# The place of ScalarE's high parts of U chunks, and the queue of one write of gates, in a decoder block with product-key experts

## The chip, the cores and the metric

The kernel runs on one core of a Trainium2 chip. The core has TensorE (PE, matmuls; its weight loads are shown apart as PEld), VectorE (DVE), ScalarE (ACT) and GpSimd (POOL), and SyncE (SP), which only issues transfers. Each engine takes its own instructions strictly in its order; semaphores join them. Transfers are issued from SP, ScalarE and GpSimd, each with its own queue. The metric is the device time of one execution in microseconds.

## The reference

One layer of a decoder: a normalised input goes through attention over a window beside gated linear attention, the sum is added to the input, and then comes the part that takes most of the time, an expert layer with product keys. Each of 512 tokens picks 16 of 16384 experts in each of 8 heads; an expert is one row of `u` and one of `v`.

```python
def block(args):
    xb, eb, gb = args                      # 128 tokens, their 128 experts, their 128 gates
    ub = jnp.take(u, eb, axis=0)
    hid = jax.nn.gelu(jnp.einsum('tkd,td->tk', ub, xb), approximate=False) * gb
    vb = jnp.take(v, eb, axis=0)
    return jnp.einsum('tk,tkd->td', hid, vb)
```

The expert indices and gates come from two top-16 searches over 128 keys each per head, the 16 best of their sums, and a softmax. At the end stands a last normalisation.

## The kernel before

**How the experts are computed.** The tokens are in four blocks of 128. For three of them (`DENSE`, 384 tokens) the kernel doesn't gather: it computes all 16384 experts with matmuls and multiplies by a dense matrix of gates that is zero where a token did not pick an expert. The last block (`GB`) is done by gathering rows, GpSimd fetching them (`gu`, `gv`) and DVE forming the products. 48 of the 384 tokens get their hidden values from gathered rows too (`spr`), so the U matmuls run over 336 tokens (`TU`).

**U chunks.** There are 128 chunks of 128 experts. A chunk c is loaded as float32 (two chunks to a transfer of 1 MB, tile `u`, a ring of three buffers), and `hilo` (L61) splits it: ScalarE writes the high part `uc<c>h` (L65), and DVE, or GpSimd early on, the low part `uc<c>l` (L66), source minus high part. Each has a ring of four buffers. `u_matmuls` (L697) does 24 matmuls (8 slices of the width, three products each: L70 high by high, L71 and L72 with the low parts) into one PSUM bank `ph`, of which there are two. `u_gelu` (L703) applies Gelu from that bank to `ge` (L706) and frees it; for the chunks of `AHEAD` the result goes to DRAM on ScalarE's queue (L708).

**Chunks ahead.** 88 of the chunks are in `AHEAD` and are computed before the V stage, in the order 4m, 4m+2, and from m = 20 on also 4m+1, 4m+3. The first 11 of them run during the search for experts, with a given engine for the low part (`lo_eng`). The others (`lo_eng` is None) are woven into the gate stage by `u_part` (L712). The last ones are, in this order, 116, 118, 117, 119, 120, 122, 121, 123, 124, 126, 125, 127. The other 40 chunks, odd ones from 1 on, run in the V stage.

**The gate stage.** It makes the matrix of gates. `gate_group` (L923) treats 16 tokens in two halves; for each half DVE builds one-hots (`o12`, L917, and `o2`, L935), TensorE does 24 matmuls into two banks `pg` (L942), and ScalarE evicts each bank to `gs` (L944). 24 groups make 48 halves, 96 evictions. In the third block (`SB`) ScalarE also copies the part for the first eight chunks to `gates_r[0]` (L949). After each odd group k the two groups in `gs` go to `Gd` in DRAM, 2 MB per write (L951): eleven writes on SP's queue and the last, k = 23, on GpSimd's. `woven` (L1186) strings the groups together with other work; in the last block it has, after groups 4 to 6, `dots_of` (two products with gathered rows on DVE) and, after groups 3 to 6, `ahead` (two fetches of such rows on GpSimd).

**The V stage.** From L1366, `prep(i)` prepares step i of the list `xs`, which begins with the U chunks 1, 3, 5, 7, 9 and then mixes V chunks and odd U chunks. For a U step it has ScalarE write the high part (L1372), runs `activate` (Gelu of gathered products), `gather_to(due[i])` (gathers and products up to a planned number, here the products of rows 6 and 7 at first), DVE's low part (L1385) and `loads(i)`. For a V step it multiplies the gates by the hidden values (L1377) and splits A and V in the same way (L1378, L1380, L1385, L1389); then 36 matmuls go into the six `acc` banks. `load_u` (L1300) loads two odd U chunks on SP's queue; three such loads stand before `prep(0)`.

**What sets the order.** DVE and GpSimd run in program order from the gate stage on (L1232). TensorE, ScalarE and SP are ordered by a scheduler's simulation up to L1246, and in program order after it; but their instructions of the V stage may be placed among the last ones of the gate stage. `tc.issue_after(ins)` adds no semaphore: each instruction traced within it on the engine of `ins` must come later than `ins` in that engine's order.

Of the kernel before, what the change touches and what calls it, by code (L numbers as in the profile page):

```python
# [12 lines left out]
AF = mybir.ActivationFunctionType  # L13
# [34 lines left out]
def peer_block_kernel(ctx: ExitStack, tc: tile.TileContext, a: dict, out: bass.AP):  # L48
# [663 lines left out]
    def u_part(c, lo_eng=None, after=None):  # L712

        j = c // 2 % 2
        if j == 0:
            u_load(c)
        uh, ul = hilo(u_part.raw[c % 2][:, j], [P, KD, P], f"uc{c}", lo_eng or nc.vector)
        with tc.issue_after(after.ins) if after is not None else nullcontext():
            ph, end = u_matmuls(c, uh, ul)
        u_gelu(c, ph)  # L720
        return end

    u_part.raw = {}

# [198 lines left out]
    def gate_group(bi, n, q):  # L923
# [5 lines left out]
        for t0 in range(0, TG, TB):  # L929
# [7 lines left out]
            for f in range(TB // 4):  # L937
                pt = bank(f"pg{n}{q}{t0}{f}", BK[f]).rearrange("p (a b) -> p a b", a=4)
                for i in range(4):
                    g, r = divmod(4 * f + i, 2)  # L940
                    for m in range(3):
                        nc.tensor.matmul(pt[:, i, :], o12[:, g, 0, :, r], o2[:, g, m, :, r],  # L942
                                         start=(m == 0), stop=(m == 2))
                nc.scalar.activation(gs[:, :, q % 2, :, t0 + 4 * f:t0 + 4 * f + 4].rearrange("p c i a -> p a c i"),  # L944
                                     pt.rearrange("p a (c i) -> p a c i", c=P // CG), AF.Copy)
            yield 1.68, 1.4
# [3 lines left out]
        if q % 2:  # L950
            (nc.gpsimd if k == NGRP - 1 else nc.sync).dma_start(Gd[:, :, k - 1:k + 1].rearrange("c p g e -> p c (g e)"),  # L951
                                                                gs.rearrange("p c g i t -> p c (g i t)"))

    gate_group.next = None
    gates_r = {}

# [214 lines left out]
    def chain(*gens):  # L1171
        for g in gens:
            yield from g
# [12 lines left out]
    def woven(n, rows, extra, rest=()):  # L1186
        for q in range(P // TG):
# [8 lines left out]
            if q in extra:  # L1196
                yield from chain(*extra[q])

    def breath():
# [166 lines left out]
    def prep(i, extra=()):  # L1366
# [14 lines left out]
        activate()  # L1381
        gather_to(due[i])
        for piece in extra:
            piece()
        nc.vector.tensor_tensor(l, src, h, OP.subtract)  # L1385
        if k == "u":
            ready[i] = h, l
# [100 lines left out]
    end = step["v", P - LAST]  # L1488
    prep(0)
    prep(1)  # L1490
    for i in range(end):
# [112 lines left out]
```

## Time and profile before

| | |
|---|---|
| median of 3 runs | 1478.58 us (1477.78 to 1479.39) |
| the profiled execution | 1486.71 us |
| its span, first to last instruction | 1484.9 us |
| mean granted TensorE clock in it | 0.989 |
| VectorE's waits for the gathered rows `gu`, `gv` | 8.1 and 5.2 us in all |
| evictions of gates (L944) | 96, 1110 ns each |
| Gelus of U chunks (L706) | 128, 440 ns each |
| high parts in the V stage (L1372), from the timeline | 1.06 us each |

A row of the page's groups reads: line, engine, operation, what it writes from what, count, then busy us, mean ns of one, idle time before it and who ended that. The profile is of one execution, which is longer than the runs without a profile. Roughly, attention and mixing take up to 280 us, the search for experts to 420 us, the gate stage to 800 us and the V stage the rest.

### The profile page before, as it was taken

What the parts mean: (1) busy time and instruction counts of PE and PEld (TensorE: products, weight loads), DVE (VectorE), ACT (ScalarE), POOL (GpSimd) and SP (SyncE); (2) the same over time, 40 slices, a digit from 0 to 9 for tenths busy, and PEclk for the clock granted to TensorE, in tenths of its full rate; (3) what the DMA queues carried; (4) which work ended last, traced back from release to release, by engine and by line L of the source; (5) the groups of instructions that cost most, each with busy time, mean ns of one, the idle gap of its engine ahead of it and who ended that gap; (6) DMA issues with size and microseconds to landing.
All of it is one profiled execution on the core that took longest, in us unless ns stands there. A gap on an engine that the chain in (4) does not pass through costs nothing.

```text
span 1484.9 us, 24692 instructions
## 1 busy us (share of the span) xinstructions
PE 1425.7 (96%) x9395; PEld 1268.4 (85%) x9395; DVE 1282.5 (86%) x2495; ACT 685.7 (46%) x1084; POOL 540.7 (36%) x374
## 2 busy tenths in 40 slices
PE   3999999899999999999998999999999999999997
PEld 3688777798899999999998888888888888888886
DVE  7577756769999899989885899999999999999997
ACT  5445475543344465555764433343333334333334
POOL 1000000044431444421022565666666657544520
PEclk9999899999999999999999999999999999999999
DMA  9262507344246899987789999999999999999971
GB/s 345 93 220 100 201 29 255 121 159 178 98 160 236 298 326 328 361 319 249 275 270 362 414 412 407 404 413 396 375 410 405 390 408 411 410 411 412 410 301 71
DMA packets 131607, 439.56 MB, mean 296 GB/s; under 512 B 13072, under 2 KB 51232, under 8 KB 110880
## 3 DMA queue, kind: packets, MB, share of 16 engines
q1 hardware_dynamic: 74080, 260.55, 46.3%
q0 software_dynamic: 44304, 161.50, 28.4%
q10 hardware_dynamic: 13104, 15.93, 3.0%
q8 instruction: 73, 1.20, 0.3%
q14 instruction: 46, 0.38, 0.1%
HBM read 393.36 MB, written 44.52 MB: 295 GB/s over the span
## 4 chain that ended last, share of the span: by engine, by line
PE 76%; DVE 9%; DMA 6%; issue 4%; ACT 2%; POOL 2%; SPq 0%; POOLq 0%; DVEq 0%; ACTq 0%
PE acc L70 11%; PE acc L71 11%; PE acc L72 11%; PE ph L70 8%; PE ph L72 7%; PE ph L71 7%; PE pg L942 3%; DMA u<-in_uT_dram 2%; POOL spr L1012 2%; DMA spr<-in_u_dram,spix 1%; PE pj L72 1%; PE pj L70 1%; PE pj L71 1%; PE pn L70 1%; PE pn L71 1%
## 5 line engine op out<-in xcount | busy, mean ns | idle before, releaser
L1064 POOL DMA_INDIRECT gu<-in_u_dram,ix_u x128 | 196.1, 1532 | 201.2 <-PE pg L942 89.3
L1099 POOL DMA_INDIRECT gv<-in_vP_dram,ix_v x128 | 193.8, 1514 | 153.1 <-DVE gu L1074 56.0
L1104 DVE SCALAR_TENSOR_TENSOR gacc<-gv,hg,gacc 128x1024 f32<-128x1024 f32 x127 | 162.5, 1280 | 5.4 <-DMA gv<-in_vP_dram,ix_v 5.2
L1074 DVE SCALAR_TENSOR_TENSOR gu<-gu,h2n 128x1024 f32<-128x1024 f32 x128 | 155.6, 1219 | 8.1 <-DMA gu<-in_u_dram,ix_u 8.1
L1012 POOL DMA_INDIRECT spr<-in_u_dram,spix x48 | 81.2, 1692 | 168.4 <-DVE spr L1018 127.2
L706 ACT ACTIVATE ge<-ph 128x336 f32<-128x336 f32 x128 | 56.3, 440 | 182.1 <-PE ph L72 176.7
L1380 ACT ACTIVATE Ah<-gr 128x384 fp32r<-128x384 f32 x128 | 66.9, 522 | 115.5 <-DVE gr L1377 111.7
L1158 POOL IOTA iot<- 128x256 bf16 x1 | 1.5, 1540 | 288.4 <-DVE h2Tl L681 288.4
L944 ACT ACTIVATE gs<-pg 128x512 f32<-128x512 f32 x96 | 95.3, 1110 | 2.5 <-PE pg L942 2.0
L935 DVE TENSOR_TENSOR o<-o,gp 128x3072 bf16<-128x3072 bf16 x48 | 84.1, 1753 | 4.7 <-PE pg L942 4.7
L942 PE MATMUL pg<-o,o 128*128 128x128 bf16 x1152 | 75.4, 221 | 0.0
L942 PEld LDWEIGHTS <-o 128*128 128x128 bf16 x1152 | 68.1, 98 | 4.9 <-issue 0.2
L1389 DVE TENSOR_TENSOR Al<-gr,Ah 128x384 fp32r<-128x384 f32 x128 | 70.7, 552 | 1.3 <-DMA Gd<-gs 1.3
L1018 DVE SCALAR_TENSOR_TENSOR spr<-spr,xs 128x1024 f32<-128x1024 f32 x48 | 58.5, 1220 | 10.9 <-DMA spr<-in_u_dram,spix 10.8
L917 DVE TENSOR_TENSOR o<-iot,t 128x2048 bf16<-128x2048 bf16 x48 | 58.3, 1219 | 4.2 <-PE pg L942 4.2
L218 DVE SCALAR_TENSOR_TENSOR macc<-wa,scs,macc 128x1024 f32<-128x1024 f32 x28 | 39.7, 1416 | 6.7 <-DMA wa<-in_w_ada_dram 6.5
L1377 DVE TENSOR_TENSOR gr<-gel,gr 128x336 f32<-128x336 f32 x64 | 32.2, 503 | 0.0
L71 PE MATMUL pq<-h2Tl,wq_0h 128*128 128x512 f32 (+1 forms) x80 | 28.2, 352 | 1.2 <-DVE h2Tl L681 1.2
L70 PE MATMUL pq<-h2Th,wq_0h 128*128 128x512 f32 (+1 forms) x80 | 28.3, 355 | 1.0 <-ACT qsc L769 1.0
L72 PE MATMUL pq<-h2Th,wq_1l 128*128 128x512 f32 (+1 forms) x80 | 28.7, 358 | 0.0
L70 PE MATMUL pq<-h2Th,wq_1h 128*128 128x512 f32 (+1 forms) x80 | 28.4, 355 | 0.0
L71 PE MATMUL pq<-h2Tl,wq_1h 128*128 128x512 f32 (+1 forms) x80 | 28.4, 355 | 0.0
(2591 smaller groups left out, 5035.7 us busy)
## 6 DMA issues: line engine op xcount, KB each, us to landing
u<-in_uT_dram SPq DMA_DIRECT2D x64, 1024.0 KB
v<-in_vP_dram SPq DMA_DIRECT2D x64, 1024.0 KB
gr<-Gd SPq DMA_DIRECT2D x15, 1536.0 KB
Gd<-gs SPq DMA_DIRECT2D x11, 2048.0 KB
wa<-in_w_ada_dram SPq DMA_DIRECT2D x20, 1024.0 KB
gsp<-ge ACTq DMA_DIRECT2D x88, 168.0 KB
gel<-gsp SPq DMA_DIRECT2D x32, 336.0 KB
wi<-in_w_in_dram SPq DMA_DIRECT2D x9, 1024.0 KB
```

The costliest lines, as they stand in the source:

```text
L70: nc.tensor.matmul(acc, lh, rh, start=start, stop=False)
L71: nc.tensor.matmul(acc, lh, rl, start=False, stop=False)
L72: return nc.tensor.matmul(acc, ll, rh, start=False, stop=stop)
L935: nc.vector.tensor_tensor(o2, o12[:, :, 1, None].to_broadcast([P, H, 3, P, 2]), gp3[:, g0:g0 + H, :, None].to_broadcast([P, H, 3, P, 2]), ...
L942: nc.tensor.matmul(pt[:, i, :], o12[:, g, 0, :, r], o2[:, g, m, :, r], start=(m == 0), stop=(m == 2))
L944: nc.scalar.activation(gs[:, :, q % 2, :, t0 + 4 * f:t0 + 4 * f + 4].rearrange("p c i a -> p a c i"), pt.rearrange("p a (c i) -> p a c i", ...
L1012: nc.gpsimd.indirect_dma_start(out=sp[m], out_offset=None, in_=a["u"], in_offset=bass.IndirectOffsetOnAxis(ap=sp["ix", i][:, j:j + 1], axi ...
L1064: nc.gpsimd.indirect_dma_start(out=ur, out_offset=None, in_=a["u"], in_offset=bass.IndirectOffsetOnAxis(ap=ix_u[:, s:s + 1], axis=0))
L1074: nc.vector.scalar_tensor_tensor(ur, ur, 1.0, h2n, op0=OP.mult, op1=OP.mult, accum_out=hid[:, s:s + 1])
L1099: nc.gpsimd.indirect_dma_start(out=vr, out_offset=None, in_=a["vP"], in_offset=bass.IndirectOffsetOnAxis(ap=ix_v[:, s:s + 1], axis=0))
L1104: nc.vector.scalar_tensor_tensor(gacc, vr, hg[:, s:s + 1], gacc, op0=OP.mult, op1=OP.add)
L1389: nc.vector.tensor_tensor(grp(Al), A, grp(Ah), OP.subtract)
```

## The change

There are four edits.

1. In `u_part`, when `lo_eng` is None and more than three Gelus have been recorded, the high part is traced under `issue_after` of the Gelu four back in the list `gelus`, to which each `u_part` adds its own.
2. `gate_group` keeps the second eviction of each half in `evicts`; `prep(0)` and `prep(1)` are traced under `issue_after(evicts[-2])`, which is the second eviction of the last half but one. That binds their ScalarE instructions, the high parts of chunks 1 and 3.
3. The write of gates for k = 21 (`NGRP - 3`) is issued on GpSimd's queue instead of SP's, and later in the program: `woven` pops it after the extra pieces of its group, so after two products on DVE and two fetches on GpSimd. The write for k = 23 stays where it was, as do the others.
4. In `prep`, `gather_to(due[i])` is left out at step 0 and comes after the low part at step 1. So the products of gathered rows 6 and 7 come after the low parts of chunks 1 and 3 on DVE, and their Gelu (`activate`) at the next step.

```diff
--- before.py
+++ after.py
@@ -714,12 +714,15 @@
         j = c // 2 % 2
         if j == 0:
             u_load(c)
-        uh, ul = hilo(u_part.raw[c % 2][:, j], [P, KD, P], f"uc{c}", lo_eng or nc.vector)
+        with tc.issue_after(gelus[-4].ins) if len(gelus) > 3 and lo_eng is None else nullcontext():
+            uh, ul = hilo(u_part.raw[c % 2][:, j], [P, KD, P], f"uc{c}", lo_eng or nc.vector)
         with tc.issue_after(after.ins) if after is not None else nullcontext():
             ph, end = u_matmuls(c, uh, ul)
         u_gelu(c, ph)
+        gelus.append(last_gelu["u"])
         return end
 
+    gelus = []
     u_part.raw = {}
 
     def u_ahead(upto, lo_eng=None):
@@ -941,17 +944,22 @@
                     for m in range(3):
                         nc.tensor.matmul(pt[:, i, :], o12[:, g, 0, :, r], o2[:, g, m, :, r],
                                          start=(m == 0), stop=(m == 2))
-                nc.scalar.activation(gs[:, :, q % 2, :, t0 + 4 * f:t0 + 4 * f + 4].rearrange("p c i a -> p a c i"),
-                                     pt.rearrange("p a (c i) -> p a c i", c=P // CG), AF.Copy)
+                evict = nc.scalar.activation(gs[:, :, q % 2, :, t0 + 4 * f:t0 + 4 * f + 4].rearrange("p c i a -> p a c i"),
+                                             pt.rearrange("p a (c i) -> p a c i", c=P // CG), AF.Copy)
+            evicts.append(evict)
             yield 1.68, 1.4
         k = bi * (P // TG) + q
         if bi == len(DENSE) - 1:
             nc.scalar.activation(gates_r[0][:, k], gs[:, 0, q % 2], AF.Copy)
         if q % 2:
-            (nc.gpsimd if k == NGRP - 1 else nc.sync).dma_start(Gd[:, :, k - 1:k + 1].rearrange("c p g e -> p c (g e)"),
-                                                                gs.rearrange("p c g i t -> p c (g i t)"))
+            writes.append(lambda: (nc.gpsimd if k >= NGRP - 3 else nc.sync).dma_start(
+                Gd[:, :, k - 1:k + 1].rearrange("c p g e -> p c (g e)"), gs.rearrange("p c g i t -> p c (g i t)")))
+            if k != NGRP - 3:
+                writes.pop()()
 
     gate_group.next = None
+    evicts = []
+    writes = []
     gates_r = {}
 
     def first_gates():
@@ -1195,6 +1203,8 @@
                     yield 0.15, 0
             if q in extra:
                 yield from chain(*extra[q])
+            if writes:
+                writes.pop()()
 
     def breath():
         nc.vector.scalar_tensor_tensor(junk[:, :2], ident[:, :2], 1.0, ident[:, :2], op0=OP.mult, op1=OP.mult,
@@ -1379,10 +1389,13 @@
             Ah, Al = make_A(f"Ah{c}"), make_A(f"Al{c}")
             nc.scalar.activation(grp(Ah), A, AF.Copy)
         activate()
-        gather_to(due[i])
+        if i > 1:
+            gather_to(due[i])
         for piece in extra:
             piece()
         nc.vector.tensor_tensor(l, src, h, OP.subtract)
+        if i == 1:
+            gather_to(due[i])
         if k == "u":
             ready[i] = h, l
         else:
@@ -1486,8 +1499,9 @@
     load_u()
     load_u()
     end = step["v", P - LAST]
-    prep(0)
-    prep(1)
+    with tc.issue_after(evicts[-2].ins):
+        prep(0)
+        prep(1)
     for i in range(end):
         if i + 2 < len(xs):
             prep(i + 2, extras.get(i + 2, ()))
```

## The prediction, made before the result was known

> **What bounds the kernel now.** I read the page's busy shares, then TensorE's list of waits from 400 us to the end, then stretches of 2 us around the longest wait, then the timelines of the engines there. The list of waits has engine and line, what was waited for, and the total, the count and the longest in us. The windows have the stretch, its length, busy us of PE, PEld, DVE, ACT and POOL, then the granted clock, the DMA share and GB/s.
>
> ```profile
> PE 1425.7 (96%) x9395; PEld 1268.4 (85%) x9395; DVE 1282.5 (86%) x2495; ACT 685.7 (46%) x1084; POOL 540.7 (36%) x374
> ...
> PE ph L70 <- ACT ge L706: 8.5, 4, 5.5
> PE ph L72 <- DVE uc120l L66: 0.7, 1, 0.7
> ...
> 790.00:792.00 2.00, 0.00 (x0) 0.00 (x0) 0.33 (x1) 0.93 (x1) 0.00 (x0) 0.56 0.99 410
> 792.00:794.00 2.00, 0.54 (x2) 0.50 (x2) 0.90 (x2) 2.00 (x4) 0.00 (x0) 0.50 1.04 432
> ...
> 796.00:798.00 2.00, 2.00 (x18) 2.00 (x16) 2.00 (x4) 2.00 (x5) 0.00 (x0) 0.73 0.29 105
> 798.00:800.00 2.00, 2.00 (x15) 2.00 (x15) 0.92 (x2) 1.43 (x4) 0.69 (x1) 1.00 0.40 51
> ```
>
> TensorE is the bound: 96% busy, and from 400 us on its list holds 8.5 us for Gelus of ScalarE, 0.7 us for a low part of DVE, and hardly more. The clock fell to half in the longest wait and was whole again only at 798 us. So a wait removed here should move all that follows, and the longest is worth more than its 5.5 us.
>
> Here is who kept whom in the two long waits, from the timelines (start, us, engine, line, operation, and in brackets the idle time before it and its releaser).
>
> ```profile
> 607.07 1.56 PE L942 MATMUL pg<-o,o 128*128 128x128 bf16 x24
> 611.01 0.42 PE L70 MATMUL ph<-h2Th,uc92h 128*128 128x336 f32 x1 [2.38 <-ACT ge L706]
> ...
> 609.56 1.06 ACT L65 ACTIVATE uc93h<-u 128x1024 fp32r<-128x1024 f32 x1 [4.59 <-DMA u<-in_uT_dram]
> 610.52 0.43 ACT L706 ACTIVATE ge<-ph 128x336 f32<-128x336 f32 x1
> ...
> 779.47 1.57 PE L942 MATMUL pg<-o,o 128*128 128x128 bf16 x24
> 784.61 1.57 PE L942 MATMUL pg<-o,o 128*128 128x128 bf16 x24
> 785.98 0.40 PE L70 MATMUL ph<-h2Th,uc125h 128*128 128x336 f32 x1
> 786.37 1.56 PE L942 MATMUL pg<-o,o 128*128 128x128 bf16 x24
> 793.46 0.65 PE L70 MATMUL ph<-h2Th,uc127h 128*128 128x336 f32 x1 [5.53 <-ACT ge L706]
> ...
> 800.43 0.31 PE L72 MATMUL ph<-h2Th,uc127l 128*128 128x336 f32 x1
> 803.80 0.32 PE L70 MATMUL ph<-h2Th,uc1h 128*128 128x336 f32 x1
> ...
> 780.57 2.04 ACT L944 ACTIVATE gs<-pg 128x512 f32<-128x512 f32 x2 [0.46 <-PE pg L942]
> 791.07 1.06 ACT L1372 ACTIVATE uc1h<-u 128x1024 fp32r<-128x1024 f32 x1 [8.45 <-DMA u<-in_uT_dram]
> 792.98 0.43 ACT L706 ACTIVATE ge<-ph 128x336 f32<-128x336 f32 x1
> ```
>
> In both, ScalarE stands idle at the high part of a U chunk whose data has not landed (4.59 and 8.45 us), and the Gelu that would free TensorE's PSUM bank stands behind it. TensorE has two such banks, so chunk 92 needs the Gelu of chunk 89, which in the list order of the chunks is four back from 93; chunk 127 needs that of 126. The second wait also holds back the evictions of the last two blocks of gate matmuls.
>
> **The end of the gate stage.** The change puts the high parts of chunks 1 and 3 behind the evictions of the last block but one. Then the Gelu of 126 runs when its matmuls end (about 785 us), and TensorE goes on at full clock after the block at 786.37: 1.37 for that block (784.61 to 785.98), 0.39 for the first pair of chunk 127 (785.98 to 786.37), 1.37 for the last block, then the remaining 22 matmuls each of chunks 125 and 127, 3.37 apiece (800.43 to 803.80). 786.37 + 1.37 + 0.39 + 1.37 + 3.37 + 3.37 = 796.24, where chunk 1 began at 803.80 before: **7.5 us** less, 5.53 of wait and the rest slow clock. What is late next must be looked at on DVE, SP and POOL:
>
> ```profile
> 771.28 1.22 DVE L66 TENSOR_TENSOR uc123l<-u,uc123h 128x1024 fp32r<-128x1024 f32 x1
> 787.51 1.22 DVE L66 TENSOR_TENSOR uc125l<-u,uc125h 128x1024 fp32r<-128x1024 f32 x1
> 788.64 1.22 DVE L66 TENSOR_TENSOR uc127l<-u,uc127h 128x1024 fp32r<-128x1024 f32 x1
> 795.24 1.23 DVE L1074 SCALAR_TENSOR_TENSOR gu<-gu,h2n 128x1024 f32<-128x1024 f32 x1 [2.35 <-DMA gu<-in_u_dram,ix_u]
> 796.39 1.22 DVE L1385 TENSOR_TENSOR uc1l<-u,uc1h 128x1024 fp32r<-128x1024 f32 x1
> ...
> 819.02 0.56 DVE L1389 TENSOR_TENSOR Al<-gr,Ah 128x384 fp32r<-128x384 f32 x1 [1.33 <-DMA Gd<-gs]
> ...
> SPq L951 <- ACT gr L949: 13.5, 1, 13.5
> ...
> 762.19 0.33 SPq L695 DMA_DIRECT2D u<-in_uT_dram  x1
> 775.78 0.37 SPq L951 DMA_DIRECT2D Gd<-gs  x1
> 776.25 13.96 SPq L1303 DMA_DIRECT2D u<-in_uT_dram  x3
> ...
> 770.64 1.06 ACT L65 ACTIVATE uc125h<-u 128x1024 fp32r<-128x1024 f32 x1 [3.39 <-DMA u<-in_uT_dram]
> ...
> 781.31 1.18 POOL L1064 DMA_INDIRECT gu<-in_u_dram,ix_u  x1 [5.72 <-PE pg L942]
> 799.31 1.22 POOL L951 DMA_DIRECT2D Gd<-gs  x1 [15.58 <-ACT gs L944]
> 819.20 1.19 POOL L1099 DMA_INDIRECT gv<-in_vP_dram,ix_v  x1 [9.39 <-DMA Gd<-gs]
> ...
> 822.20 0.39 PE L70 MATMUL acc<-vc0h,Ah 128*128 128x512 f32 x1
> ```
>
> The low part of 125 ends at 788.73 and is wanted at 789.50; that of 127 ends at 789.86 and is wanted at 792.87. Both hold, the first by 0.8 us, so DVE is next in line and little more than 7.5 us is to be had here.
>
> **The high part's own data.** SP sat 13.5 us at the second last write of gates, which waits for evictions, and the load of chunks 1 and 3 stood behind it until 776.25. Its buffer came free with the low part of 123 at 772.50, so without that write it leaves 3.75 us earlier and without 2 MB before it. It took 14.8 us (776.25 to 791.07); the load before took 8.45 (762.19 to 770.64). Landing is thus between 781.0 and 787.3. A block's two evictions end 3.1 us after its matmuls begin (780.57 + 2.04 less 779.47), so those ahead of the high parts end at 786.37 + 3.1 = 789.5. Data no longer decides: 789.5 + 1.06 + 1.22 is 791.8 for the low part of chunk 1, wanted at 796.5.
>
> **The gathers' order on DVE.** Before, the low part of chunk 1 began at 796.39, behind the product with the gathered row that arrived late (a wait of 2.35 us). At 796.39 it would now be the next stall, of about 1.1 us. The edit puts the two low parts first, so it costs nothing; the products come after, and their Gelu one step later, with no reader before the first V steps.
>
> **The write on POOL.** It is issued behind two gathers, waits for the same evictions (775.78) and takes 1.22 us of POOL, as the one such row shows; the next gather starts at 781.31, for it waits for TensorE. That is 4.3 us of cover, and only gathers stand behind it. If the evictions were later by more than that, the gathers of rows 6 and 7 would slip, and behind them DVE's low part of chunk 5, wanted only at about 803.9. Their data now queues behind 2 MB. The only POOL write needed 19.9 us from issue to the wait it ended (799.31 to 819.20); at that price the gathers land by about 796 to 798, still in time. The last write moves up too: its evictions end near 792.7, and 19.9 us later is 813, where the first V matmul now comes at 822.20 - 7.5 = 814.7, its Al 0.56 behind the write. A margin of 1 us at the dearest price; I cost both at nothing.
>
> The Trainium skill speaks against this edit: SBUF — State Buffer, section "SBUF: two separate sides", says that GpSimd can't write a DMA's descriptors while DVE holds their shared port in a two-port mode, and gives about 3.1 us instead of 0.62 for such a transfer. By it the write would hold POOL to about 779.2, an estimate, and the sum would be the same; no run here shows a write beside a busy DVE.
>
> **The Gelu four back.** It orders the high parts of 77 chunks (88 in the list less 11 issued before). For chunk 93 it lets the Gelu go at once: **2.38 us**, at full clock. The other 0.6 us of Gelu waits I leave at nothing gained; the ends are 0 and 0.6. Its price: a high part comes later by one Gelu, 0.43 us, at most by the two evictions as well, 2.5 us. DVE takes low parts in a fixed order, so one-hots and products stand behind a late one. One such wait is on record, and it bears on both sides, since DVE also waits for TensorE:
>
> ```profile
> 660.36 1.23 DVE L66 TENSOR_TENSOR uc104l<-u,uc104h 128x1024 fp32r<-128x1024 f32 x1 [1.43 <-ACT uc104h L65]
> 712.81 1.76 DVE L935 TENSOR_TENSOR o<-o,gp 128x3072 bf16<-128x3072 bf16 x1 [3.38 <-PE pg L942]
> ```
>
> The 3.38 us of DVE idling at 712.81 show that DVE can follow a TensorE that is 2.4 us early. For late high parts I take 0.43 us once, nearest to the one row; the ends are 0 and 2.5.
>
> The sum: 7.5 + 2.4 - 0.4 = **9.5 us**. The profiled execution took 1486.71 us with a span of 1484.9; the median of the runs is 1478.58, 8.1 us less. No term is a share of the span, so I take the difference off the median: **1469.1 us**. The lower end is 7.5 + 2.4 + 0.6 + 0.7 (the wait for the low part of 120) + 0.8 for the spread of the runs (1478.58 to 1477.78): 12.0, or 1466.6.
>
> **The rivals.**
>
> *Only the end gains.* The order of TensorE, ScalarE and SP in this stage comes from a scheduler's simulation, and new edges can shift it; DVE, 0.8 us behind at the end, may keep what chunk 93 gives. For it speaks the 0.7 us wait for chunk 120, against it the 3.38 us above. 1478.6 - 7.5 = 1471.1. Chance 0.14.
>
> *The V stage is bound by DMA and takes it back.*
>
> ```profile
> 1110.00:1160.00 50.00, 50.00 (x253) 43.96 (x252) 47.20 (x64) 19.39 (x27) 33.47 (x21) 1.00 0.99 392
> ```
>
> The DMA share is 0.99 there, and in the windows above only 796 to 800 had DMA to spare: 2 x 0.71 + 2 x 0.60 = 2.6 us. If all else were full, the gain could not exceed that and the write's head start, say 3.4: 1475.2. Against it: TensorE waits for nothing there. DMA: Bandwidth & Descriptors, section "Specifications", of the Trainium skill puts the ceiling at 435 GB/s, for this rival; the 392 above is below it. Chance 0.10, half of it beyond 0.2%.
>
> *The change doesn't do what it says*: the scheduler puts other unlanded high parts, or the last blocks of gates, ahead of the Gelus that TensorE needs. 1478.6, chance 0.06.
>
> *Slower: late high parts on DVE.* If Gelu and evictions both pass ahead of each high part, the waits that DVE now has once come often. 77 chunks at 0.2 us each reach 15.4 us: 1478.6 - 9.5 + 15.4 = 1484.5. It takes the gain from 0.12 us a chunk on and is slower than 0.2% from 0.16. For it: DVE is 86% busy over all. Against: one wait of the kind so far. Chance 0.08.
>
> **The numbers.** The forecast holds 0.62, from 1466.6 to about 1471.5. 0.2% is 3.0 us, about what a measurement of this kernel can tell from no change. Faster: 0.62 + 0.14 + half of 0.10, 0.81; within: the other half + 0.06, 0.11; slower: 0.08. The range goes up to 1475.5, which takes in the first rival and half of the second.
>
> **What would show it.** TensorE's waits for Gelu should fall from 8.5 to under 1 us; the granted clock should stay at 1.00 from 780 to 810; chunk 93's high part should stand behind its Gelu; the high parts of 1 and 3 behind all but two evictions and without a DMA wait; SP's load for them some 3.7 us earlier against the low part of 123; chunk 1 on TensorE about 9.9 us earlier, and the V stage as long as before. I am wrong if DVE's waits for high parts grow past 5 us, or if TensorE shows a new wait behind chunk 127 or for the first V chunks.

## The result, and the profile after the change

The changed kernel takes 1470.68 us (median; 1466.74 to 1475.86) beside 1479.45 us (1475.53 to 1484.54) for the kernel before on the same chip: a ratio of 0.9939, with a 95% interval from 0.9923 to 0.9956, 8.8 us less. The forecast was 1469.1.

The profiled execution took 1471.75 us with a span of 1470.0. Its line numbers are those of the changed code: Gelu is still L706, a gate matmul L945, an eviction L947, a write of gates L955, a high part of the V stage L1382, a low part of gates L1402, a product with a gathered row L1082, the load of U chunks L1313. First the page's busy shares, then TensorE's list of waits from 400 us on, in the columns of the prediction.

```profile
PE 1417.9 (96%) x9395; PEld 1262.6 (86%) x9395; DVE 1280.1 (87%) x2495; ACT 684.1 (47%) x1084; POOL 542.2 (37%) x375
```

```profile
PE ph L72 <- DVE uc123l L66: 1.2, 1, 1.2
PE acc L72 <- DVE Al L1402: 0.7, 1, 0.7
PE ph L72 <- DVE uc120l L66: 0.6, 1, 0.6
PE trg L892 <- ACT xs L987: 0.5, 1, 0.5
PE ph L72 <- DVE uc22l L66: 0.3, 1, 0.3
```

The 8.5 us of waits for Gelu are gone. Three waits are new: 1.2 us for the low part of chunk 123 and 0.7 us for the first gates of the V stage, both for DVE, and 0.5 us for ScalarE at a transpose (`trg`). The last one, 0.5 us each time, is in all nine profiles with the first edit and in none of the five without it.

**What may be compared.** The two profiled spans differ by 14.9 us, more than the medians do. Here are the first matmul with the low part of chunk 22 and the first one of the last V chunk, in the timeline of before and then of after:

```profile
435.41 0.42 PE L72 MATMUL ph<-h2Th,uc22l 128*128 128x336 f32 x1 [0.31 <-DVE uc22l L66]
...
1463.06 0.39 PE L70 MATMUL acc<-vc127h,Ah 128*128 128x512 f32 x1
```

```profile
429.25 0.43 PE L72 MATMUL ph<-h2Th,uc22l 128*128 128x336 f32 x1 [0.31 <-DVE uc22l L66]
...
1448.05 0.39 PE L70 MATMUL acc<-vc127h,Ah 128*128 128x512 f32 x1
```

Chunk 22 is among the first that the edits touch, and it comes 6.16 us earlier already. The windows show one part of this: from 100 to 200 us the granted clock was 0.91 in before and 0.97 in after (second fence), while a second profile of the same changed kernel, after_again below, had 0.93 there and came to chunk 22 at 431.04.

```profile
100.00:200.00 100.00, 95.86 (x1426) 80.34 (x1424) 70.51 (x170) 50.95 (x141) 0.00 (x0) 0.91 0.46 160
```

```profile
100.00:200.00 100.00, 95.26 (x1448) 79.84 (x1447) 72.72 (x177) 51.67 (x142) 0.00 (x0) 0.97 0.46 160
```

So the change is measured from chunk 22 to the last V chunk: 1463.06 - 435.41 = 1027.65 us before and 1448.05 - 429.25 = 1018.80 after, **8.85 us** less, as the medians say. Later in this text, "the stretch" is this length, and each kernel's is read from its own profile in the same way.

**The two stalls of before, in the profile after** (timelines of ScalarE, SP and GpSimd):

```profile
600.59 1.05 ACT L65 ACTIVATE uc93h<-u 128x1024 fp32r<-128x1024 f32 x1
...
776.32 0.45 ACT L706 ACTIVATE ge<-ph 128x336 f32<-128x336 f32 x1 [2.23 <-PE ph L72]
...
779.40 2.01 ACT L947 ACTIVATE gs<-pg 128x512 f32<-128x512 f32 x2
781.17 1.09 ACT L1382 ACTIVATE uc1h<-u 128x1024 fp32r<-128x1024 f32 x1
782.14 1.08 ACT L1382 ACTIVATE uc3h<-u 128x1024 fp32r<-128x1024 f32 x1
783.08 2.05 ACT L947 ACTIVATE gs<-pg 128x512 f32<-128x512 f32 x2
...
764.10 17.70 SPq L1313 DMA_DIRECT2D u<-in_uT_dram  x3
...
767.20 1.23 POOL L955 DMA_DIRECT2D Gd<-gs  x1 [3.46 <-ACT gs L947]
772.98 1.14 POOL L1072 DMA_INDIRECT gu<-in_u_dram,ix_u  x1 [4.55 <-PE pg L945]
785.42 1.21 POOL L955 DMA_DIRECT2D Gd<-gs  x1 [10.07 <-ACT gs L947]
```

No high part has a bracket of idle time before it: neither that of chunk 93 nor that of chunk 1 waits for its load. The latter stands between the last two blocks' evictions. Its load leaves SP at 764.10, 0.03 us after the low part of chunk 123 (762.85 + 1.22), where before it left 3.75 us after it. In the windows, TensorE is busy throughout between 780 and 800 us at a clock of 1.00 (first fence: before, 14.46 us busy and 0.83; second: after). The end of the gate stage comes some 16 us earlier in after, and its window from 770 to 790 us also has 20.00 us busy and 1.00.

```profile
780.00:800.00 20.00, 14.46 (x138) 13.78 (x136) 14.74 (x23) 10.52 (x15) 2.81 (x3) 0.83 0.90 344
```

```profile
780.00:800.00 20.00, 20.00 (x144) 20.00 (x142) 10.18 (x13) 11.15 (x17) 8.85 (x8) 1.00 0.98 370
```

**The two new waits for DVE** (timelines of DVE and TensorE in after):

```profile
761.70 1.23 DVE L1082 SCALAR_TENSOR_TENSOR gu<-gu,h2n 128x1024 f32<-128x1024 f32 x1 [1.21 <-DMA gu<-in_u_dram,ix_u]
762.85 1.22 DVE L66 TENSOR_TENSOR uc123l<-u,uc123h 128x1024 fp32r<-128x1024 f32 x1
764.13 0.42 PE L72 MATMUL ph<-h2Th,uc123l 128*128 128x336 f32 x1 [1.15 <-DVE uc123l L66]
...
766.26 1.75 DVE L938 TENSOR_TENSOR o<-o,gp 128x3072 bf16<-128x3072 bf16 x1
...
806.91 0.56 DVE L1402 TENSOR_TENSOR Al<-gr,Ah 128x384 fp32r<-128x384 f32 x1 [5.22 <-DMA Gd<-gs]
807.52 0.50 PE L72 MATMUL acc<-vc0h,Al 128*128 128x512 f32 x1 [0.70 <-DVE Al L1402]
```

At 761.70 DVE waits 1.21 us for a gathered row that belongs to a product, and the low part that TensorE wants stands behind the product. At 806.91 it waits for the last write of gates, issued at 785.42: 21.5 us.

### The profile page after: what moved, and what is told of

It reads as the page before. It is cut to its first block, busy times and chain, and to the rows that moved or that the text cites. A ratio compares the mean times of both kernels' runs of the same rounds, so it can differ in the third digit from the quotient of the medians.

```text
span 1470.0 us, 24660 instructions
## 1 busy us (share of the span) xinstructions
PE 1417.9 (96%) x9395; PEld 1262.6 (86%) x9395; DVE 1280.1 (87%) x2495; ACT 684.1 (47%) x1084; POOL 542.2 (37%) x375
## 4 chain that ended last, share of the span: by engine, by line
PE 82%; DVE 8%; DMA 4%; issue 3%; ACT 2%; POOL 1%; SPq 0%; ACTq 0%; DVEq 0%; POOLq 0%
PE acc L72 12%; PE acc L70 12%; PE acc L71 12%; PE ph L70 9%; PE ph L72 9%; PE ph L71 9%; PE pg L945 4%; DMA Gd<-gs 1%; PE pj L72 1%; PE pj L70 1%; PE pj L71 1%; PE pn L70 1%; PE pn L71 1%; PE pn L72 1%; PE sc L395 1%
## 5 line engine op out<-in xcount | busy, mean ns | idle before, releaser
L706 ACT ACTIVATE ge<-ph 128x336 f32<-128x336 f32 x128 | 57.7, 451 | 309.8 <-PE ph L72 309.8
L1082 DVE SCALAR_TENSOR_TENSOR gu<-gu,h2n 128x1024 f32<-128x1024 f32 x128 | 155.2, 1216 | 2.9 <-DMA gu<-in_u_dram,ix_u 2.7
L947 ACT ACTIVATE gs<-pg 128x512 f32<-128x512 f32 x96 | 95.6, 1113 | 2.2 <-PE pg L945 2.2
L938 DVE TENSOR_TENSOR o<-o,gp 128x3072 bf16<-128x3072 bf16 x48 | 84.0, 1750 | 5.1 <-PE pg L945 5.0
L1402 DVE TENSOR_TENSOR Al<-gr,Ah 128x384 fp32r<-128x384 f32 x128 | 70.3, 549 | 5.2 <-DMA Gd<-gs 5.2
L945 PE MATMUL pg<-o,o 128*128 128x128 bf16 x1152 | 74.1, 220 | 0.0
L945 PEld LDWEIGHTS <-o 128*128 128x128 bf16 x1152 | 66.9, 97 | 4.6
## 6 DMA issues: line engine op xcount, KB each, us to landing
gel<-gsp SPq DMA_DIRECT2D x32, 336.0 KB, 12.2
```

Source lines behind the costliest of these rows:

```text
L938: nc.vector.tensor_tensor(o2, o12[:, :, 1, None].to_broadcast([P, H, 3, P, 2]), gp3[:, g0:g0 + H, :, None].to_broadcast([P, H, 3, P, 2]), ...
L947: evict = nc.scalar.activation(gs[:, :, q % 2, :, t0 + 4 * f:t0 + 4 * f + 4].rearrange("p c i a -> p a c i"), pt.rearrange("p a (c i) -> p ...
L1082: nc.vector.scalar_tensor_tensor(ur, ur, 1.0, h2n, op0=OP.mult, op1=OP.mult, accum_out=hid[:, s:s + 1])
L1402: nc.vector.tensor_tensor(grp(Al), A, grp(Ah), OP.subtract)
```

## The experiments

Each kernel keeps or leaves out some of the four edits: 1 the Gelu four back, 2 the anchor behind evictions, 3 the write on GpSimd's queue, 4 the order of the products. Kernels that keep only a few are diffed against before, the others against after. The table cuts each stretch at the first matmuls with the low parts of chunks 22, 121, 123 and 1, and at the first matmul of V chunk 1. From there to the last V chunk it is 636.75 or 636.76 us in every profile, so this part of the V stage never changes. A ratio is to runs of before on the same chip; the runs were on several chips.

The scheduler orders TensorE and ScalarE anew for each kernel, so an edit can move instructions that it doesn't name. With edit 1 TensorE's matmuls of the gate stage stand in another order. Without the anchor and with the write moved, the high part of chunk 1 stands ahead of the Gelu of chunk 124, while before it stands only ahead of that of chunk 126.

| kernel | edits | ratio to before [95% interval] | 22 to 121 | 121 to 123 | 123 to 1 | 1 to V 1 | stretch |
|---|---|---|---|---|---|---|---|
| before | none | | 330.39 | 6.92 | 31.39 | 22.19 | 1027.65 |
| before_again | none | 1.0 [0.9982, 1.0017] | 329.80 | 6.91 | 34.43 | 22.18 | 1030.07 |
| only_gelu | 1 | 0.9982 [0.9967, 0.9997] | 326.71 | 6.86 | 30.08 | 22.17 | 1022.58 |
| only_anchor | 2 | 0.9964 [0.9949, 0.9979] | 327.56 | 6.91 | 27.22 | 22.20 | 1020.64 |
| only_write | 3 | 0.9930 [0.9912, 0.9948] | 329.05 | 6.92 | 23.86 | 22.19 | 1018.77 |
| gelu_write | 1, 3 | 0.9928 [0.9911, 0.9945] | 327.04 | 7.95 | 23.97 | 22.19 | 1017.90 |
| no_gelu | 2, 3, 4 | 0.9955 [0.9935, 0.9974] | 331.44 | 6.91 | 23.86 | 22.78 | 1021.74 |
| no_anchor | 1, 3, 4 | 0.9936 [0.9918, 0.9955] | 326.71 | 6.85 | 23.97 | 22.19 | 1016.47 |
| write_on_sp | 1, 2, 4 | 0.9950 [0.9933, 0.9966] | 327.11 | 8.47 | 23.98 | 22.88 | 1019.20 |
| products_first | 1, 2, 3 | 0.9956 [0.9939, 0.9973] | 327.27 | 7.84 | 23.96 | 22.20 | 1018.02 |
| after | all | 0.9939 [0.9923, 0.9956] | 326.73 | 8.15 | 23.97 | 23.20 | 1018.80 |
| after_again | all | 0.9936 [0.9914, 0.9959] | 326.72 | 8.18 | 23.96 | 22.90 | 1018.51 |
| split_last | 1, 3, 4 and more | 0.9985 [0.9969, 1.0001] | 326.72 | 8.26 | 23.98 | 30.06 | 1025.77 |
| last_write_act | all and more | 1.0059 [1.0035, 1.0082] | 326.72 | 8.30 | 23.98 | 39.32 | 1035.08 |

**One edit alone: the Gelu** (against before).

```diff
-        uh, ul = hilo(u_part.raw[c % 2][:, j], [P, KD, P], f"uc{c}", lo_eng or nc.vector)
+        with tc.issue_after(gelus[-4].ins) if len(gelus) > 3 and lo_eng is None else nullcontext():
+            uh, ul = hilo(u_part.raw[c % 2][:, j], [P, KD, P], f"uc{c}", lo_eng or nc.vector)
...
+        gelus.append(last_gelu["u"])
```

> Only the first edit: each high part of a U chunk behind the Gelu four chunks back; the anchor, the write and the products are as before the change. Theory: the wait of 2.4 us at chunk 92 goes, as does the one of 0.5 us at chunk 87, and the 5.5 us wait at the end of the gate stage stays, with its slow clock. Counted from the first matmul with a low part of chunk 22, TensorE reaches chunk 93 some 3.0 us earlier than before the change and chunk 1 some 2 to 3 us earlier; ratio 0.998. Rival (DVE takes it back): chunk 93 is earlier but chunk 126 isn't; ratio 1.000.

The wait at chunk 92 is gone and that at chunk 127 is not; ScalarE's timeline, and TensorE's list of waits:

```profile
600.36 1.05 ACT L65 ACTIVATE uc93h<-u 128x1024 fp32r<-128x1024 f32 x1
...
779.51 1.06 ACT L1381 ACTIVATE uc1h<-u 128x1024 fp32r<-128x1024 f32 x1 [6.95 <-DMA u<-in_uT_dram]
```

```profile
PE ph L70 <- ACT ge L706: 4.0, 1, 4.0
```

So the two stalls are separate, and this edit ends the first one only. The one at the end was 4.0 us here, not 5.5: the load ended ScalarE's wait 12.2 us after its issue at 767.31, against 14.8 before.

**One edit alone: the anchor** (against before).

```diff
-    prep(0)
-    prep(1)
+    with tc.issue_after(evicts[-2].ins):
+        prep(0)
+        prep(1)
```

> Only the second edit: the high parts of chunks 1 and 3 behind the second eviction of the last half but one. Theory: the 5.5 us wait for a Gelu and its slow clock go (7.5 us), but the load of chunks 1 and 3 still stands behind the write on SP and lands where it did, so the high part of chunk 1 still waits for it, the last two evictions wait with it, and its low part stands behind the products of rows 6 and 7: a new wait of about 1 us on TensorE at chunk 1 and one of 1 to 2 us at the first V chunk, behind the last write. Net gain 4 to 6 us, ratio 0.996 to 0.997. Rival (the anchor does it alone, edits three and four are worth nothing): 7.5 us less 1, ratio 0.9956, no wait at chunk 1.

The stall at the end goes, but 3.1 us come back at chunk 1, more than the 1 us expected. Timelines of TensorE, ScalarE, DVE and GpSimd:

```profile
788.16 0.42 PE L70 MATMUL ph<-h2Th,uc1h 128*128 128x336 f32 x1 [3.10 <-ACT ge L706]
...
787.68 0.43 ACT L706 ACTIVATE ge<-ph 128x336 f32<-128x336 f32 x1
...
785.35 1.23 DVE L1081 SCALAR_TENSOR_TENSOR gu<-gu,h2n 128x1024 f32<-128x1024 f32 x1 [3.62 <-DMA gu<-in_u_dram,ix_u]
...
771.43 0.94 POOL L1071 DMA_INDIRECT gu<-in_u_dram,ix_u  x1 [0.30 <-issue]
```

A gathered row took 13.9 us (771.43 to 785.35), DVE's product waited for it, the Gelu of the products waits for DVE, and behind that and a high part stands the Gelu of chunk 125 on ScalarE, which frees the bank for chunk 1. A stall at this place was foreseen in the prediction, but through the low part of chunk 1 on DVE; it came through ScalarE. The expected wait for the first V chunk did not come: the last write landed in 9.4 us.

**One edit left out: the write** (against after).

```diff
-            writes.append(lambda: (nc.gpsimd if k >= NGRP - 3 else nc.sync).dma_start(
+            writes.append(lambda: (nc.gpsimd if k == NGRP - 1 else nc.sync).dma_start(
                 Gd[:, :, k - 1:k + 1].rearrange("c p g e -> p c (g e)"), gs.rearrange("p c g i t -> p c (g i t)")))
-            if k != NGRP - 3:
-                writes.pop()()
+            writes.pop()()
```

> All but the third edit: the write of gates for k = 21 stays on SP's queue. Theory: the load of chunks 1 and 3 leaves after that write, 3 to 4 us later than in the changed kernel, and the high part of chunk 1 waits for it for 1 to 2 us on ScalarE; TensorE doesn't wait at chunk 1, but the last evictions and with them the last write are later by as much, and the wait at the first V chunk (0.7 us in the changed kernel) grows to 2. Ratio 0.995. Rival one (the write's queue is free): as the changed kernel, 0.994, no DMA wait of the high part. Rival two: with one write less on GpSimd's queue the last one lands sooner than its 21.5 us, and the wait at the first V chunk goes; 0.993.

The timelines of SP and ScalarE:

```profile
771.69 2.07 SPq L1312 DMA_DIRECT2D u<-in_uT_dram  x1
...
785.72 1.07 ACT L1381 ACTIVATE uc1h<-u 128x1024 fp32r<-128x1024 f32 x1
```

The theory fell, and rival one's sign is there: the load left SP behind the write at 771.23, and yet the high part of chunk 1 waited for no data. With the anchor the load was in time here even from behind the write; in the run with the anchor alone the high part waited 0.9 us for it, which held up no matmul. The wait at the first V chunk is 0.4 us, not 2. The ratio can't be told from that of the whole change: the intervals overlap.

**One edit left out: the order of the products** (against after).

```diff
-        if i > 1:
-            gather_to(due[i])
+        gather_to(due[i])
...
-        if i == 1:
-            gather_to(due[i])
```

> All but the fourth edit: the products of gathered rows 6 and 7 come before the low parts of chunks 1 and 3 on DVE, as before the change. Theory of the prediction: the products wait for their rows as they did (about 2 us), the low part of chunk 1 is late, and TensorE has a new wait of about 1 us at chunk 1; ratio 0.9947. Rival: in the changed kernel the rows have landed by then, since they are fetched 8 us earlier against TensorE's end of the stage; no new wait, ratio 0.994.

The rows came in time: the two products began at 779.91 and 781.23, the low part of chunk 1 behind them ended at 783.6, and TensorE took it up at 785.88 without a wait, as the rival had it. So the edit was not needed here; it could help only in an execution whose rows come late, as in the run with the anchor alone, and no run tries it on such rows. Without it the last write landed in 17.6 us (783.18 to 800.81), and TensorE had no wait for the gates.

**One edit left out: the anchor** (against after).

```diff
-    with tc.issue_after(evicts[-2].ins):
-        prep(0)
-        prep(1)
+    prep(0)
+    prep(1)
```

> All but the second edit: nothing ties the high parts of chunks 1 and 3. In this kernel's order on ScalarE the high part of chunk 1 stands even ahead of the Gelu of chunk 124. Theory: its load leaves after the low part of 123 and lands some 9 to 15 us later; ScalarE idles there, the Gelu of 124 and two evictions wait, and TensorE has a wait of 2 to 6 us for a Gelu, with slow clock if it is a long one; against chunk 22 chunk 1 is 3 to 6 us earlier than before the change instead of 9.9. Ratio 0.996 to 0.998. Rival (the earlier load alone is enough, the anchor is worth nothing): ratio 0.994, no wait for a Gelu over 0.5 us.

My theory fell. I had expected a Gelu wait of 2 to 6 us, and there is none. The high part of chunk 1 does stand ahead of a Gelu, that of 124, but its data is there (timelines of SP and ScalarE):

```profile
763.63 17.71 SPq L1313 DMA_DIRECT2D u<-in_uT_dram  x3
...
770.55 1.06 ACT L1382 ACTIVATE uc1h<-u 128x1024 fp32r<-128x1024 f32 x1 [0.87 <-PE ph L71]
771.51 0.43 ACT L706 ACTIVATE ge<-ph 128x336 f32<-128x336 f32 x1
```

What it waits for is TensorE. The load landed in at most 6.9 us (763.63 to 770.55); from behind the write it had taken 14.8. From the gate stage on TensorE, DVE, GpSimd and SP have the same order of work as in after; only ScalarE's differs, in the places of the high parts of chunks 1 and 3 and two issues. This raised the question whether the write alone would do, which the later runs answer.

**One edit left out: the Gelu** (against after).

```diff
-        with tc.issue_after(gelus[-4].ins) if len(gelus) > 3 and lo_eng is None else nullcontext():
+        with tc.issue_after(gelus[-4].ins) if False else nullcontext():
```

> All but the first edit: high parts as before the change, ahead of the Gelu four back. Theory of the prediction: the wait of 2.4 us at chunk 92 is back, ratio 0.9955. Rival: that wait hangs on how long one load of 1 MB takes (17.6 us in the profile of before; with the anchor alone it landed in time and there was no such wait), so it may be absent in this profile, and the first edit is worth 0 to 3 us from run to run; ratio between 0.994 and 0.9955.

The stall at chunk 92 is back as the theory had it (ScalarE's and TensorE's timelines):

```profile
605.88 1.06 ACT L65 ACTIVATE uc93h<-u 128x1024 fp32r<-128x1024 f32 x1 [4.65 <-DMA u<-in_uT_dram]
...
607.33 0.42 PE L70 MATMUL ph<-h2Th,uc92h 128*128 128x336 f32 x1 [2.43 <-ACT ge L706]
```

**No edit: before, once more.**

> The kernel before once more, unchanged, for a second profile. Theory: both waits of TensorE for Gelus are there, 2.4 us at chunk 92 and 5.5 us at chunk 127. Rival: the first one varies with the landing of one load and may be anywhere from 0 to 3 us, the second is there with 4 to 6 us. Ratio 1.000; the spread of the ratio about 1 tells what differences can be read from times. The start of the gate stage (the first low part of chunk 22) may come at another time than 435.4 us, since the profiles of the other kernels show it from 427 to 433.

The ratio is 1.0 [0.9982, 1.0017]. The stretch is 2.4 us longer than in the first profile, and from chunk 123 to chunk 1 it is 3.0 longer: there TensorE waited 7.5 us, for a high part whose load came 17.0 us after its issue at 772.25 (ScalarE's timeline):

```profile
789.22 1.06 ACT L1372 ACTIVATE uc1h<-u 128x1024 fp32r<-128x1024 f32 x1 [10.45 <-DMA u<-in_uT_dram]
```

So one profile of before is good to 2 or 3 us at this place, and the ratios are needed.

**One edit more: the last write on ScalarE's queue** (against after).

```diff
-            writes.append(lambda: (nc.gpsimd if k >= NGRP - 3 else nc.sync).dma_start(
+            writes.append(lambda: (nc.scalar if k == NGRP - 1 else nc.gpsimd if k == NGRP - 3 else nc.sync).dma_start(
```

> The changed kernel with the last write of gates (k = 23) on ScalarE's queue instead of GpSimd's; nothing else. Theory: the write took 21.5 us on GpSimd's queue because it shares the engines with the loads on SP's queue and the gathers behind it; on a third queue it gets its own turn, lands in 10 to 16 us, and the waits for it go: DVE's 5.2 us at the first Al, TensorE's 0.7 us, GpSimd's 10.7 us. TensorE gains 1 us from the first V chunk on: ratio 0.9932, not to be told from 0.9939 by times, only by the rows. Rival: the engines are full (413 GB/s) and the write takes 20 us on any queue; the waits stay.

DVE's wait for the last write goes, as meant, but the kernel is slower than before. ScalarE's and TensorE's timelines:

```profile
788.17 0.38 ACTq L955 DMA_DIRECT2D Gd<-gs  x1
790.10 18.23 ACTq L708 DMA_DIRECT2D gsp<-ge  x1
...
808.38 0.21 ACT L1091 ACTIVATE hg<-hid 128x8 f32<-128x8 f32 x1 [18.31 <-issue]
...
808.98 0.65 PE L70 MATMUL ph<-h2Th,uc3h 128*128 128x336 f32 x1 [14.32 <-ACT ge L706]
```

A small transfer issued on the same queue behind the 2 MB, 0.33 us at other times, held ScalarE for 18.23 us; the Gelus stood behind it and TensorE idled 14.32 us.

**One edit alone: the write** (against before).

```diff
-            (nc.gpsimd if k == NGRP - 1 else nc.sync).dma_start(Gd[:, :, k - 1:k + 1].rearrange("c p g e -> p c (g e)"),
-                                                                gs.rearrange("p c g i t -> p c (g i t)"))
+            writes.append(lambda: (nc.gpsimd if k >= NGRP - 3 else nc.sync).dma_start(
+                Gd[:, :, k - 1:k + 1].rearrange("c p g e -> p c (g e)"), gs.rearrange("p c g i t -> p c (g i t)")))
+            if k != NGRP - 3:
+                writes.pop()()
...
+            if writes:
+                writes.pop()()
```

> Only the second last write of gates goes to GpSimd's queue; the places of the high parts and the order of the products are those of before, so uc1h stands in front of Gelu of 124 and uc93h in front of Gelu of 89. Theory (the load of U chunk 1 was late because 2 MB stood in front of it on SP's queue): with the write gone from that queue the load is issued about 3.7 us earlier and lands within about 7 us, before uc1h's turn; no wait for the Gelu of 124 to 126, TensorE never idles for more than 1 us between chunks 121 and 126, its clock stays at 1.00 there. The 2.4 us wait at chunk 92 stays in profiles where chunk 93's load is late. At chunk 1 a wait of 0 to 3.4 us for Gelu of 125, which stands behind hg and the high part of chunk 5 (as in the run with the anchored high parts alone). Gain from chunk 22 on 4 to 8 us, ratio 0.9945 to 0.9975. Rival (the place of uc1h on ScalarE is what matters, the write only moves the load by some us): a Gelu wait of 4.0 to 5.5 us at chunks 124 to 127 stays, ratio 0.998 to 1.000.

This one edit has the whole gain: a ratio of 0.9930, and 8.9 us of the stretch, more than the 4 to 8 expected. TensorE's list of waits, then the timelines of ScalarE and SP:

```profile
PE ph L70 <- ACT ge L706: 1.7, 2, 1.6
```

```profile
601.52 1.06 ACT L65 ACTIVATE uc93h<-u 128x1024 fp32r<-128x1024 f32 x1 [3.83 <-DMA u<-in_uT_dram]
...
771.47 1.06 ACT L1382 ACTIVATE uc1h<-u 128x1024 fp32r<-128x1024 f32 x1 [1.97 <-PE ph L71]
...
764.49 17.71 SPq L1313 DMA_DIRECT2D u<-in_uT_dram  x3
```

The load lands within 7.0 us (764.49 to 771.47), and the stall at the end is gone without the anchor. The expectation was wrong in one thing: the high part of chunk 1 is not where it stood before. It stands earlier, ahead of the Gelu of 124 and two evictions. That new place can't have ended the stall by itself, since a late load would hold up ScalarE there sooner still; it is the data that came in time. The 1.6 us that are left are those of chunk 92.

**Two edits: Gelu and write** (the two diffs above together, against before).

> High parts behind the Gelu four chunks back, and the second last write on GpSimd's queue; the anchor behind gate evictions and the new order of the products are left out. Theory (either the anchor or the write removes the stall at the end, the Gelu rule removes that at chunk 92, and the order of the products is needed only when rows are late): no Gelu wait above 0.5 us anywhere, gain from chunk 22 on 8.5 to 11 us, ratio 0.9925 to 0.995, the same as the whole change. Rival (the order of the products matters): Gelu of 125 stands behind hg on ScalarE and TensorE waits 2 to 3.4 us at chunk 1, gain 5.5 to 8, ratio 0.995 to 0.997.

The ratio, 0.9928, is that of the write alone and of the whole change on the same chip (0.9930 and 0.9936). The order of the products wasn't needed: no Gelu wait is left at chunk 1. ScalarE's timeline shows how near the data is here:

```profile
767.74 1.06 ACT L1382 ACTIVATE uc1h<-u 128x1024 fp32r<-128x1024 f32 x1 [2.29 <-DMA u<-in_uT_dram]
```

The high part of chunk 1 waits 2.29 us for a load that took 7.3 us, and TensorE has no wait from it. How much later the load could be was not tried; in other profiles with the write moved it took up to 8.3 us.

**Edits 1, 3 and 4, and the last two groups of gates written each by itself** (against the kernel without the anchor).

```diff
-        if q % 2:
+        if k >= NGRP - 2:
+            nc.gpsimd.dma_start(Gd[:, :, k:k + 1].rearrange("c p g e -> p c (g e)"),
+                                gs[:, :, q % 2].rearrange("p c i t -> p c (i t)"))
+        elif q % 2:
```

> The whole change without the anchor, and with the last two groups of gates written each by itself, so that the last write carries 1 MB in place of 2 MB. Theory (the wait for Al at the first V chunk is the landing of the last 2 MB, 19.5 to 21.5 us): the last write lands 10 to 15 us after its issue, before DVE comes to Al, the waits of DVE at Al (1.6 to 5.2 us) shrink below 1 us and TensorE has none there; gain from chunk 22 on 9 to 11.5 us, ratio 0.9915 to 0.994. Rival (the two halves queue behind each other and the last lands when the whole would have): the wait at Al stays as it was, ratio 0.9935 to 0.995. Second rival (one more write holds GpSimd's queue and so the gathers of V rows): the first gv is later than 810 us and TensorE waits at the first V chunks, ratio above 0.995.

This was meant to better the change and lost nearly all of it. GpSimd's, DVE's and TensorE's timelines:

```profile
777.98 1.18 POOL L955 DMA_DIRECT2D Gd<-gs  x1 [11.55 <-ACT gs L947]
779.47 1.08 POOL L1075 DMA_INDIRECT gu<-in_u_dram,ix_u  x1 [0.30 <-PE pg L945]
780.85 1.94 POOL L1075 DMA_INDIRECT gu<-in_u_dram,ix_u  x1 [0.30 <-DVE uc1l L1399]
782.77 1.24 POOL L955 DMA_DIRECT2D Gd<-gs  x1
...
793.30 1.23 DVE L1085 SCALAR_TENSOR_TENSOR gu<-gu,h2n 128x1024 f32<-128x1024 f32 x1 [2.31 <-DMA gu<-in_u_dram,ix_u]
...
795.51 0.65 PE L70 MATMUL ph<-h2Th,uc3h 128*128 128x336 f32 x1 [5.65 <-ACT ge L706]
```

The wait of the new write stands on GpSimd: 11.55 us for evictions, with two fetches of rows behind it. In no_anchor they went at 772.50 and 773.95, 15.7 and 17.2 us after TensorE's chunk 121; here they go 25.4 and 26.8 us after it. The rows come late, the Gelu of the products waits, and behind it the Gelu that TensorE needs. The second rival had named the cause, GpSimd held by one more write, but for the fetches of V rows; it was those of U rows. The first rival holds in part: the last half still took 18.3 us, from its issue at 782.77 to the gather that it released at 801.08.

**The whole change, once more.**

> The whole change once more. Theory: ratio 0.992 to 0.9955, no Gelu wait above 0.5 us, no wait of uc1h for its load. The waits of TensorE for the low part of chunk 123 (1.15 us) and for Al (0.70 us) are the landing of one gathered row and of one write: if they vary from run to run they come out anywhere from 0 to 1.5 us here. If instead they belong to the new order, both stand here at the same places with the same lengths within 0.3 us.

Both new waits stand at the same places, 1.2 us for chunk 123 and 0.4 for the gates (0.70 in the first profile). So they are not one unlucky landing, and belong to the order of the work at least in part.

## Why the prediction was right, and where its steps were off

The time came out in the range, 1470.68 us against 1469.1, and both stalls that were named are gone. That the sum is off by only 0.7 us is partly luck, since errors of its terms cancel: one gained 1.3 us more than its figure, and two cost 1.8 more.

**The end of the gate stage, 7.5 us: right in size, and its reason only half right.** From chunk 123 to chunk 1 the stretch went from 31.39 to 23.97 us, 7.4; the first matmul of chunk 1 comes 9.85 us earlier against chunk 22, as foreseen (9.9). Both the wait and the slow clock went. The size is that of one profile of before: by before_again it would be 10.5. But the prediction gave this to the anchor, with the write as a help to the data. The runs show two edits of which either will do: with the write moved the data is there in about 7 us, soon enough even for an earlier place of the high part (no_anchor and only_write, 23.97 and 23.86); with the anchor the place is right and the data may come later (write_on_sp, 23.98). The prediction bounded the landing between 781.0 and 787.3 and let both ends pass; it did not ask what the lower end, 8.45 us, would mean without the anchor. The anchor alone, though, gave back 3.4 us in its run, behind a gathered row that took 13.9 us; products_first, with the same order of products, has no wait there with rows that took 9.1 and 9.0.

**Chunk 92, 2.38 us: right, and larger.** The stretch from 22 to 121 is 326.7 to 327.3 us in the nine profiles with edit 1, and 327.6 to 331.4 in the five without it. Against the first profile of before it is 3.66 us. TensorE's idle time fell by 2.67 of it (3.71 to 1.04): all 3.0 us for Gelus and a little at chunk 120, less the new 0.49 for ScalarE. The other 1.0 us is busy time (326.68 to 325.69 for the same 2737 matmuls, at a clock of 1.00 in both profiles). TensorE's order of work differs with the edit; whether that shortens it was not tried. What is lost at chunk 92 without the edit depends on when one load lands: 1.6 us of wait in only_write, 2.4 in no_gelu, none in only_anchor.

**Late work on DVE, 0.4 us: the term that was mis-sized.** It came at 1.2 us, once, and not as a late high part: the product in front of the low part of 123 waited for its gathered row. The row had been fetched at 750.43 and landed 11.25 us later. Seven of nine profiles with edit 1 have a wait of 0.8 to 1.5 us there, none of the five without it. That TensorE comes to chunk 123 about 3 us earlier against rows that land as before would explain it; no run moved the fetch, so this stays an argument.

**The last write, costed at nothing with a margin of 1 us: wrong by 0.7 to 1.0.** The prediction had the low part of the gates 0.56 us behind a write of 19.9 us. It took 21.5, and 21.1 to 21.2 in the other three profiles with edits 2 and 4 and this write on GpSimd's queue. The issue was late too: the prediction's 792.7 for the end of the last evictions does not come out of its own rows, since 789.5 and two high parts of 1.06 and the evictions of 2.04 make 793.7. With the anchor the last evictions stand behind two high parts, so the write leaves 2.7 us before chunk 1 (785.42 to 788.10) instead of 4.3 (783.36 to 787.62 in no_anchor). TensorE's wait there shows in just these four profiles, 0.3 to 0.7 us. Elsewhere the same write landed in 9.4 us (only_anchor) to 19.7; why it is slowest with both edits was not tried. The prediction had named a new wait for the first V chunks as a sign that it is wrong, and this step is where it was.

**The write on GpSimd, costed at nothing: right.** It took 1.23 us, and the next fetch waited for TensorE after it, 4.55 us against the 4.3 foreseen. DVE was in a bf16 operation (L938) from 766.26 to 768.01 while GpSimd issued the write at 767.20, and the issue took no longer than the later one, 1.21 us. This is no test of the rule of the Trainium skill that the prediction weighed (SBUF — State Buffer, section "SBUF: two separate sides"): it speaks of two-port modes, and the same section says that `tensor_tensor`, which L938 is, has none.

**The rivals.** The V stage did not take the gain back: 636.75 us against 636.76. "Only the end gains" did not come true for the whole change; only_write comes near it, with 7.5 us there and 1.3 before chunk 121. Nothing of the slower rival showed: DVE's one wait for a high part in the gate stage of before (1.43 us, chunk 104) is gone in after, which has one of 0.85 us at chunk 1.

By these terms the change is 3.66 up to chunk 121, less 1.23 at chunk 123, 7.42 at the end, less 1.01 at the start of the V stage: 8.84 us of the 9.5 forecast. Each of the first three edits alone has a ratio whose interval lies below 1, and the third alone has the whole gain. It is not the only way there: without it the other three give 0.9950 [0.9933, 0.9966], which can't be told from the whole change. What edit 1 adds to the third, 2.0 us up to chunk 121 less 1.0 at chunk 123 (gelu_write beside only_write), lies inside the intervals of the ratios: no version here is shown to be faster than the write alone.

## What to carry to other kernels

When an instruction waits for its data and blocks a queue, ask two questions apart: why the data is late, and what stands behind the wait; here one moved issue mended the first, and three edits to the order were not shown to better it. Before moving a transfer to an engine that also fetches, find where its wait will stand and what it holds up: the same engine took the second last write at no cost that shows, and half of the last one, put ahead of two fetches, cost some 7 us (0.9985 beside 0.9936). Test such edits alone as well as together, since two that each cure the same stall look, in the sum, as if both were needed.

## What the runs showed of the hardware that was not expected

- **An issue can block its engine.** Behind 2 MB on ScalarE's queue the next small transfer took 18.23 us to issue, against 0.33 us for the others of that profile (last_write_act); ScalarE did nothing meanwhile.
- **A load behind a large write on one queue.** The load of chunks 1 and 3 landed in 5.1 to 8.3 us in the six profiles that tell it with nothing in front of it (only_write the shortest, after the longest), and in 11.8 to 17.0 us in the five with 2 MB of gates issued 0.5 us ahead (write_on_sp, before_again).
- **The last write of 2 MB on GpSimd's queue** took from 9.4 us (only_anchor) to 21.4 (after) to land, beside other transfers, and the last half of it, 1 MB behind another, 18.1 (split_last).
